# A two-block transformer kernel: the first attention's softmax parts, head ends, weight splits and adaptive-scale steps rearranged

## The chip, the cores and the metric

The kernel runs on one core of one Trainium2 chip. A core has a matrix engine (TensorE, PE in the profile; its weight loads are PEld), three engines for elementwise work (VectorE or DVE, ScalarE or ACT, GpSimd or POOL), a queue that only issues transfers (SyncE or SP) and 16 DMA engines. Each engine runs its own instructions in the order in which they were written and waits on semaphores for the others. The metric is the device time of one execution in microseconds: before, the median of three runs is 3294.83 us (3290.88 to 3296.75).

## What is computed

Two residual blocks over 2048 tokens of width 1024, all in float32. The change lies in the first:

```python
def first_block(x, ...):
    h = rmsnorm(x, norm_pre_g)
    q, k, v, g_attn, c_h, c_b, c_c, g_conv = split(h @ w_in)
    q, k = rope(q), rope(k)                      # 12 heads of 64
    # three windows: (128, step 1), (512, step 4), (2048, step 16), mixed by softmax of their log-sums
    o = sum_i softmax(lse)_i * dilated_window_attn(q, k, v, window_i, step_i)
    attn_out = o * silu(g_attn)
    conv_out = c_b * causal_depthwise_conv(c_c * c_h, conv_w) * silu(g_conv)
    x = x + rmsnorm(concat(attn_out, conv_out) @ w_out, norm_post_g)
```

The second block scales its norms by `silu(c) @ w_ada + b_ada` ("ada" below), then has a Fourier mix, a windowed attention and a mixture of 16 experts.

## The kernel before

Matrix products with float32 accuracy are made in one of two ways. Either both operands are cut into a rounded high part and a rest (`split`: ScalarE casts the high part, VectorE subtracts it), and the products of the parts are summed, or an operand is taken whole in float32.

**Stage A** makes the projections: `proj` is 24 products of 512 columns, four groups of tokens for each of 26 weight tiles. Between them, in the last 14 tiles, stand the ada steps: a step ends one pair of ada tiles (`Ada.end`: two small products that sum over partitions), cuts the sums of the pair before (`finish`), makes sums on VectorE (`sums`) and loads a tile. One step stands behind each group of products in tiles 0 to 8 of the 14, and two in three of the groups. What `end` multiplies was cut in the step before it. `Bias.heads` writes a 2 MB table out.

**Stage B** is the first attention, head by head (`phase_b`, 12 heads). The loop over heads holds 20 slots (`for k, ... in enumerate(ch)`), one for each chunk of up to 512 columns of the exponentials. In slot k PE transposes the chunk's four blocks into PSUM (`tpose`), then computes some scores of the next head (`score`: two products, and a VectorE instruction that adds the mask and takes the minimum); ACT makes exponentials (`expo`); `parts` brings the transposed chunk to SBUF; and PE multiplies by v the chunk of two slots before (`products(2)`, `mms`). `parts` has three ways, by a table `WHOLE` with one letter a chunk: H cuts into two parts (ACT and DVE), A and V copy the chunk whole (ACT or DVE). A whole chunk's product is one float32 instruction, a cut one's is two. Heads 0 to 10 copy 8 of 20 chunks whole, head 11 copies 7.

`total` gathers the sums of the exponentials of a head across partitions with 16 small copies on POOL (in the last head on DVE); `total2`, in slot 2 of the next head, adds, inverts, and at once transposes the inverse on PE. v is loaded in one layout and turned into the second on POOL (`turn_v`, 16 copies a head). POOL also repeats ka and kb to the other 64 partitions (`repeat`) and sorts q (`order`). The result T of a head has the sums of two halves in its upper and lower partitions: one half is stored, the other is added in DRAM by a POOL transfer (`rest`).

Heads 10 and 11 carry in addition the cuts of the eight 128x1024 tiles of `w_out` (`wo.split`: a copy and a subtraction of 1024 columns), four in each. Head 11 has no scores left to make; instead PE has the first 14 pieces of the output product (`fill`, 3 products of 512 columns each), whose left operand comes from loads (`out.loads`), multiplications on POOL and a cut (`out.mul`). Stage C begins with the other half of that product, for which nothing is missing, and then needs the next 256 tokens' operand, which `mix_loads(1)` and `mix_mul(1)` bring. All loads stand in SP's one queue.

Of the kernel before, what the change touches and what calls it, by code (L numbers as in the profile page):

```python
# [9 lines left out]
F32 = mybir.dt.float32  # L10
# [83 lines left out]
def prep(inp):  # L94
# [35 lines left out]
    "s_v": ([H1, 128, NT, 128], F32),  # L130
# [167 lines left out]
def phase_a(tc, A, K):  # L298
    nc = tc.nc
    ident, eps = K["ident"], K["eps"]  # L300
    with ExitStack() as es:
# [23 lines left out]
        with ExitStack() as e1:  # L325
# [74 lines left out]
            def v_store(t, vs):  # L400
                nc.sync.dma_start(A["s_v"][:, :, t].rearrange("h p d -> p h d"), vs.rearrange("p h a d -> p h (a d)").bitcast(F32))
# [184 lines left out]
        with tc.manual_schedule():  # L586
            last = None
            loads, sums = [], []
            na = 0

            def ada_step(more):
                nonlocal na
                ada.end()
# [11 lines left out]
            for i, j in enumerate(order):  # L605
                nxt = order[i + 1] if i + 1 < len(order) else None
                if i == 9:
# [5 lines left out]
                for n in range(4):  # L613
# [17 lines left out]
class QK:  # L631
# [10 lines left out]
    def open(self):  # L642
        self.add(1)
        with self.tc.using_default_side("right"):
            self.q2p = self.es.enter_context(self.tc.tile_pool(name="q2B", bufs=2, reuse_waits="tile"))
# [12 lines left out]
    def repeat(self, h, n, eng):  # L658

        t = self.T[h][n]  # L660
# [23 lines left out]
class Out:  # L684
# [19 lines left out]

    def mul(self, tiles, hl, ks, eng):
        raw, g, r = tiles
        if ks.start < 6:
            eng.tensor_mul(g[:, ks], g[:, ks], r[:, ks])
            eng.tensor_mul(raw[:, ks], raw[:, ks], g[:, ks])
        split(self.tc.nc, hl[0][:, ks], hl[1][:, ks], raw[:, ks])  # L710
# [15 lines left out]
def phase_b(tc, A, K):  # L726
# [5 lines left out]
    with ExitStack() as es:  # L732
# [18 lines left out]
        m2 = cp.tile([128, 512], F32, name="m2")  # L751
        HD = {}
# [3 lines left out]
        def load_v(h):  # L756
            v1, v2 = (vv[h % 2].tile([128, KC, 256], F32R, name=n).rearrange("p a b -> p (a b)") for n in ("ph", "pl"))
            v1, v2 = v1.rearrange("p (t d) -> p t d", d=128), v2.rearrange("p (c a d) -> p c a d", c=4, d=128)
            nc.sync.dma_start(v1.bitcast(F32), A["s_v"][h])
            HD.setdefault(h, {}).update(v1=v1, v2=v2)  # L760

        def turn_v(h, i):

            d, (c, u) = HD[h], divmod(i, 4)
            nc.gpsimd.tensor_copy(d["v2"][QD[u], c], d["v1"][QD[c], u::4].bitcast(F32))
# [44 lines left out]
        WHOLE = [{k: {"A": nc.scalar.copy, "V": nc.vector.tensor_copy}[e] for k, e in enumerate(w) if e != "H"} for w in ("HAHHAHHHHHAHVHVVHHVA", "VVHAVHVVHHVHHHHHHHHH")]  # L810
# [20 lines left out]
        def total(h):  # L831
            d = HD[h]
            L = d["den"]
            E = st.tile([128, 4, 4], F32, name="E2", bufs=2)
# [1734 lines left out]
```

## Time and profile before

| | |
|---|---|
| median of the runs (lowest to highest) | 3294.83 us (3290.88 to 3296.75) |
| the profiled execution: its own time, its span | 3293.63 us, 3291.8 us |
| PE busy | 3110.4 us, 94% of the span |
| DVE, ACT, POOL busy | 2021.7, 1437.4, 675.4 us (61%, 44%, 21%) |
| stage A until | 754 us |
| stage B: first scores, first slot of head 0, of head 10, of head 11 | 754, 772.0, 1079.4, 1112.6 us |
| last product of head 11, first product of the next tokens | 1157.9, 1179.3 us |

The page's shares are averages over the span. Four places matter here: the ada steps in stage A (430 to 630 us), the steady heads (772 to 1079), heads 10 and 11, and the seam to stage C (1158 to 1185).

### The profile page before, as it was taken

To read this page: it belongs to the slowest core of one execution; us is meant where nothing else is said; L and a number is where in the kernel's file an instruction comes from. 1 tells how busy PE (TensorE), PEld (TensorE's weight loads), DVE (VectorE), ACT (ScalarE), POOL (GpSimd) and SP (SyncE) were. 2 spreads that over 40 slices of the span, in tenths; PEclk is the share of its full clock that TensorE was granted. 3 is DMA by queue.
4 is the path that set the end of the run, shared out by engine and by line. 5 is a ranking of instruction groups with operands and counts; after the bars stand their busy time and mean duration, and the time that the engine had idled before them with its cause. 6 is when DMAs were issued, how large, how long until landed. Compare 5 with 4: busy or idle time off the path is not lost. (4 is left out here: it accounts for less than half of the span.)

```text
span 3291.8 us, 49939 instructions
## 1 busy us (share of the span) xinstructions
PE 3110.4 (94%) x19200; PEld 2766.1 (84%) x19200; DVE 2021.7 (61%) x4077; ACT 1437.4 (44%) x3072; POOL 675.4 (21%) x784
## 2 busy tenths in 40 slices
PE   9999999999999889789998999489999999999998
PEld 8988877888888767689986778389999999999997
DVE  5445557627888835547777476755565665565654
ACT  4322211105888723436657332244444444454443
POOL 0022210005566447311121010100110010010010
PEclk9999999999999999899999999789999999999999
DMA  5433357405555478544444765346666556665653
GB/s 167 138 132 122 117 184 233 142 20 143 148 126 142 117 218 232 140 132 154 146 139 153 235 187 175 129 180 212 211 211 213 205 205 212 211 217 206 208 203 102
DMA packets 200885, 556.83 MB, mean 169 GB/s; under 512 B 26512, under 2 KB 119580, under 8 KB 180294
## 3 DMA queue, kind: packets, MB, share of 16 engines
q1 hardware_dynamic: 186902, 499.73, 45.3%
q0 software_dynamic: 13456, 53.37, 7.0%
q8 instruction: 151, 2.47, 0.3%
q14 instruction: 88, 0.72, 0.1%
q10 hardware_dynamic: 288, 0.53, 0.0%
HBM read 425.29 MB, written 130.37 MB: 169 GB/s over the span
## 5 line engine op out<-in xcount | busy, mean ns | idle before, releaser
L2481 PE MATMUL mm<-xh,wh 128*128 128x256 f32 x2048 | 581.9, 284 | 0.2 <-ACT xh L188 0.2
L2481 PE MATMUL mm<-xl,wh 128*128 128x256 f32 x2048 | 580.7, 284 | 0.1
L2481 PE MATMUL mm<-xh,wl 128*128 128x256 f32 x2048 | 580.5, 283 | 0.0
L2475 DVE TENSOR_TENSOR wl<-raw,wh 128x1024 fp32r<-128x1024 f32 x380 | 453.8, 1222 | 177.0 <-ACT wh L2474 177.0
L2481 PEld LDWEIGHTS mm<-xh,wh 128*128 128x128 f32 x2048 | 394.2, 192 | 1.1 <-ACT xh L188 0.4
L2481 PEld LDWEIGHTS mm<-xl,wh 128*128 128x128 f32 x2048 | 394.1, 192 | 1.0 <-DVE xl L189 0.4
L2481 PEld LDWEIGHTS mm<-xh,wl 128*128 128x128 f32 x2048 | 394.1, 192 | 0.0
L2474 ACT CAST wh<-raw 128x1024 fp32r<-128x1024 f32 x384 | 390.1, 1049 | 0.0
L481 PE MATMUL mm<-hH,wl 128*128 128x512 f32 x832 | 325.2, 391 | 1.9 <-DVE wl L189 1.9
L481 PE MATMUL mm<-hH,wh 128*128 128x512 f32 x832 | 325.6, 391 | 0.0
L481 PE MATMUL mm<-hL,wh 128*128 128x512 f32 x832 | 325.4, 391 | 0.0
L2536 POOL DMA_INDIRECT out_dram<-yo,idx x32 | 63.1, 1973 | 750.7 <-DVE yo L2535 583.0
L829 ACT ACTIVATE s<-s,nm 128x256 f32<-128x256 f32 (+3 forms) x384 | 202.1, 531 | 19.5 <-DVE nm L824 19.5
L189 DVE TENSOR_TENSOR pl<-pt,ph 128x512 fp32r<-128x512 f32 (+1 forms) x269 | 176.6, 662 | 48.7 <-ACT ph L188 46.6
L2531 PE MATMUL y<-wh,hh 128*128 128x512 f32 x512 | 204.4, 399 | 0.0
L2531 PE MATMUL y<-wh,hl 128*128 128x512 f32 x512 | 200.1, 391 | 0.0
L2531 PE MATMUL y<-wl,hh 128*128 128x512 f32 x512 | 199.7, 390 | 0.0
L188 ACT CAST ph<-pt 128x512 fp32r<-128x512 f32 (+1 forms) x269 | 149.8, 562 | 110.4 <-PE pt L856 40.9
L481 PEld LDWEIGHTS mm<-hH,wl 128*128 128x128 f32 x832 | 157.2, 189 | 35.2 <-DVE wl L189 2.3
L481 PEld LDWEIGHTS mm<-hH,wh 128*128 128x128 f32 x832 | 157.1, 189 | 35.2 <-issue 1.7
L481 PEld LDWEIGHTS mm<-hL,wh 128*128 128x128 f32 x832 | 157.0, 189 | 32.2
L798 DVE CUSTOM_DVE_ANT_0 s<-ps,m 128x256 f32<-128x256 f32 (+3 forms) x384 | 156.9, 449 | 35.2 <-PE ps L797 33.8
(474 smaller groups left out, 6938.1 us busy)
## 6 DMA issues: line engine op xcount, KB each, us to landing
raw<-in_wg SPq DMA_DIRECT2D x32, 2048.0 KB
raw<-in_wd SPq DMA_DIRECT2D x32, 2048.0 KB
raw<-in_wu SPq DMA_DIRECT2D x31, 2048.0 KB
adaw<-in_wada SPq DMA_DIRECT2D x32, 768.0 KB
x<-in_x SPq DMA_DIRECT2D x32, 512.0 KB
wraw<-in_w1t SPq DMA_DIRECT2D x26, 512.0 KB
s_v<-vs SPq DMA_DIRECT2D x16, 768.0 KB
q<-s_q SPq DMA_DIRECT2D x12, 1024.0 KB
```

Source lines behind the costliest of these rows:

```text
L188: nc.scalar.copy(hi, src)
L189: (e or nc.vector).tensor_tensor(lo, src, hi.bitcast(F32), op=ALU.subtract)
L481: nc.tensor.matmul(p, a[:, k, :], b[:, k, tk], start=i == 0, stop=i == 3 * KC - 1)
L798: nc.vector.tensor_tensor_reduce(sv, p[:, :w], mask[:, mask.shape[1] - w:], 1.0, TOP, ALU.add, ALU.min, d["nm"][:, i:i + 1])
L829: nc.scalar.activation(sv, sv, AF.Exp, bias=d["nm"][:, i:i + 1], scale=-1.0, accum_out=d["den"][:, i:i + 1])
L2474: nc.scalar.copy(hi[:, c], RAW[i][:, c])
L2475: eng.tensor_tensor(lo[:, c], RAW[i][:, c], hi[:, c].bitcast(F32), op=ALU.subtract)
L2481: nc.tensor.matmul(p, a.rearrange("p (k f) -> p k f", k=KC)[:, k, w0:w0 + 128], b[:, k, :], start=i == 0, stop=i == 3 * KC - 1)
L2531: nc.tensor.matmul(ys[sl][:, cs], a[:, kk, sl * 128:sl * 128 + 128], b[:, k, cs], start=kk == 0 and j == 0, stop=kk == 7 and j == 2)
L2536: nc.gpsimd.indirect_dma_start(out=A["out"], out_offset=bass.IndirectOffsetOnAxis(ap=idx[:, sl:sl + 1], axis=0), in_=y, in_offset=None, co ...
```

## The change

- **ada**: one step a group in tiles 0 to 9, none doubled; `end` takes what was cut two steps before (`aged`). `Bias.heads` goes to tile 9.
- **v**: stored by four transfers a tile in the second layout, and loaded in both layouts (1 MB each a head, five transfers); `turn_v` is gone.
- **parts**: the table `PARTS` has new letters: P copies whole on ACT, Q on DVE, into a new tile `pw`, and POOL then cuts it (a cast and a subtraction). Heads 0 to 10: 12 H, 5 P, 3 Q, none whole. Head 11: 11 H, 6 Q, 3 A (whole). Products follow three slots later (`products(3)`), what follows a product one slot later (`leave`).
- **total** is 16 small products on PE in slot 2; `total2` (slot 3) adds and inverts on DVE; `total3` (slot 5) transposes.
- Scores are spread over 15 slots instead of 14; `repeat` comes in eight quarters; `q2` has one buffer instead of two; `rest` goes from slot 6 to slot 15 (9 and 6 in heads 10, 11); T is copied by DVE three times of four (before, ACT three times).
- **All eight weight cuts in head 11**, copies by ACT and DVE in turn, subtractions on DVE.
- **End of head 11**: PE adds T's halves (four products with `both`), so the POOL transfer and the x5 load go; the reciprocals are spread by two products. `fill` begins at slot 8, its last two pieces stand behind the loop. `mix_mul(1)` is on DVE.

```diff
-                if i == 9:
+                if i == 10:
@@ ada_step
-                ada.end()
+                if ada.late and aged:
+                    ada.end()
+                aged = bool(ada.late)
@@ stage A, after each group
-                    if i < 9 and i * 4 + n > 1:
-                        for _ in range(1 + (i in (2, 4, 6) and n == 0)):
-                            ada_step(na < 32)
-                        if i == n == 1:
+                    if i < 10 and i * 4 + n > 2:
+                        ada_step(na < 32)
+                        if i == 9 and n == 1:
                             bias.heads(ps)
@@ phase_b
-        WHOLE = [... for w in ("HAHHAHHHHHAHVHVVHHVA", "VVHAVHVVHHVHHHHHHHHH")]
+        PARTS = ("HPHPHPHPHHPHHQHHQHQH", "QHQAQHQHHQAHQHHHHHAH")
@@ total
-            for c in range(4):
-                for u in range(4):
-                    copy(E[QD[c], u, :], Lr[QD[u], 1, c, :])
+            for u in range(4):
+                for c in range(4):
+                    nc.tensor.matmul(E[QD[c], u, :], ident[:, QD[u]], Lr[:, 1, c, :], start=True, stop=True, skip_group_check=True)
@@ parts
+            if how in "PQ":
+                whole = pw[:, k // 2 % 4, :w]
+                (nc.scalar.copy if how == "P" else nc.vector.tensor_copy)(whole, p[:, :w])
+                nc.gpsimd.tensor_copy(hi[:, :w], whole)
+                nc.gpsimd.tensor_tensor(lo[:, :w], whole, hi.bitcast(F32)[:, :w], op=ALU.subtract)
+            else:
+                split(nc, hi[:, :w], lo[:, :w], p[:, :w])
@@ the loop over heads
-            LA, SC, JD = 1, 14, 1
+            LA, SC = 1, 15
-            L10, W10, W11 = (4, 13), (8, 9, 16, 17), (4, 6, 8, 10)
+            AT = {H1 - 2: 9, H1 - 1: 6}
+            W11, L11 = {0: 0, 1: 1, 3: 2, 5: 3, 7: 4, 9: 5, 12: 6, 16: 7}, {5: 6, 8: 7}
-            MU, FB = {4: slice(6, 8), 9: slice(0, 2), 10: slice(2, 4), 11: slice(4, 5)}, 6
+            TM = {6: slice(0, 2), 8: slice(2, 4), 10: slice(4, 5)}
+            MU, FB = {4: slice(6, 8), 9: slice(0, 2), 13: slice(2, 4), 15: slice(4, 5)}, 8
-                    products(2)
+                    products(3)
-                    if k == 2 and h:
-                        total2(h - 1)
-                    if k == 6 and h:
+                    if h and k in (2, 3, 5):
+                        (total, total2, None, total3)[k - 2](h - 1)
+                    if h and k == AT.get(h, 15):
                         HD[h - 1].pop("rest")()
@@ behind the loop
-            nc.vector.tensor_mul(x5, x5, g5)
-            split(nc, hl[0][:, 5], hl[1][:, 5], x5)
+            for q in range(4):
+                p = ps_t.tile([128, 512], F32, name="pt")
+                nc.tensor.matmul(p[own], both, T[:, q * 512:q * 512 + 512], start=True, stop=True)
+                if q == 0:
+                    nc.vector.tensor_mul(x5[own], p[own, :256], g5[own])
+                    split(nc, hl[0][:, 5], hl[1][:, 5], x5)
+                nc.scalar.copy(T[own, q * 512:q * 512 + 512], p[own])
+            nc.sync.dma_start(A["s_t"][5, own], T[own])
@@ mix_mul
-                out.mul(tiles, parts, slice(k, k + 2), nc.gpsimd)
+                out.mul(tiles, parts, slice(k, k + 2), nc.vector if pi == 1 else nc.gpsimd)
```

PE in slots 2 and 3 of head 5, before (pt: a transposed chunk, ps: scores, po: products with v):

```order
L876 MATMUL po<-pl,ph 128x256
L848 MATMUL pt<-ident,r 16x128
L856 MATMUL pt<-ident,s_7859 128x128 x4
L797 MATMUL ps<-ka,q_8132 128x512
L797 MATMUL ps<-kb,q_8132 128x512
L797 MATMUL ps<-ka,q_8132 128x128
L797 MATMUL ps<-kb,q_8132 128x128
L876 MATMUL po<-ph 128x256
L876 MATMUL po<-ph 128x128
L856 MATMUL pt<-ident,s_7859 128x128 x4
```

and the same engine there after the change, from slot 2 on:

```order
L853 MATMUL pt<-den,ident 32x4 x16
L871 MATMUL pt<-ident,s_8003 128x128 x4
L811 MATMUL ps<-ka,q_8352 128x384
L811 MATMUL ps<-kb,q_8352 128x384
L811 MATMUL ps<-ka,q_8352 128x512
L811 MATMUL ps<-kb,q_8352 128x512
L897 MATMUL po<-ph 128x256
L897 MATMUL po<-pl,ph 128x256
L897 MATMUL po<-ph 128x256
L897 MATMUL po<-pl,ph 128x256
```

The transposition of the inverse (`L848`) has left slot 2, sixteen small products stand there, and the products without a second row (a whole chunk) have become pairs.

POOL over one steady head, before (pl<-ph: `turn_v`, E<-den: `total`):

```order
L905 DMA s_t<-T 64x2048
L661 CAST ka<-ka 64x2048
L661 CAST kb<-kb 64x2048
L765 CAST pl<-ph 32x512 x2
L777 COPY q_8132<-q 128x512 x4
L765 CAST pl<-ph 32x512 x4
L839 COPY E_8250<-den 32x4 x16
L765 CAST pl<-ph 32x512 x10
```

and after, the middle of such a head (ph, pl<-pw: the cut of a P or Q chunk):

```order
L886 CAST ph<-pw 128x512
L887 TENSOR_TENSOR pl<-pw,ph 128x512
L667 CAST ka<-ka 64x512 x2
L886 CAST ph<-pw 128x256
L887 TENSOR_TENSOR pl<-pw,ph 128x256
L667 CAST kb<-kb 64x512 x3
L791 COPY q_9356<-q 128x512
L886 CAST ph<-pw 128x256
L887 TENSOR_TENSOR pl<-pw,ph 128x256
L667 CAST kb<-kb 64x512
L791 COPY q_9356<-q 128x512
L922 DMA s_t<-T 64x2048
```

The cuts stand between quarters of the repeats, so that PE's products now wait for POOL too.

SP's queue at the seam, before (s_t: the stored T; raw, g, r: the next tokens' operand):

```order
L902 DMA m_5772<-T 64x256
L904 DMA s_t<-T 64x2048
L697 DMA raw<-s_mix 128x2x256
L699 DMA g<-s_g 128x4x256
L702 DMA r<-s_r 64x4x256 x2
```

and after:

```order
L866 DMA s_r<-rt 16x128
L1110 DMA s_t<-T 64x2048
L703 DMA raw<-s_mix 128x2x256
L705 DMA g<-s_g 128x4x256
L708 DMA r<-s_r 64x4x256 x2
```

The store of T, which now holds the summed halves, stands ahead of the loads as the store of one half did before; the load of x5 from T is gone.

## Rows read from the trace of the kernel before

**Rows 1.** Windows: head 0 to 9, head 10, head 11; first row names columns.

```profile
core 0: us, PE busy (x) PEld busy (x) DVE busy (x) ACT busy (x) POOL busy (x), PEclk, DMA share, GB/s
772.00:1079.40 307.40, 293.81 (x2374) 263.72 (x2375) 259.87 (x896) 259.72 (x840) 205.25 (x410) 0.99 0.52 138
1079.40:1112.60 33.20, 29.81 (x239) 26.53 (x238) 29.08 (x94) 25.84 (x85) 15.94 (x28) 1.00 0.46 128
1112.60:1157.90 45.30, 36.20 (x193) 29.37 (x192) 31.80 (x60) 25.00 (x75) 19.70 (x18) 0.89 0.37 104
```

**Rows 2.** Timeline of PE in head 4: start, us, line, out<-in, idle before.

```profile
901.75 0.27 PE L848 MATMUL pt<-ident,r 128*16 128x128 f32 x1 [1.32 <-DVE r L846]
```

**Rows 3.** Timeline of PE: products of chunks whole (x4) and cut, and what follows.

```profile
904.68 0.28 PE L876 MATMUL po<-ph 128*128 128x256 f32 x1
...
905.15 0.60 PE L856 MATMUL pt<-ident,s 128*128 128x128 f32 x4
...
908.45 1.02 PE L876 MATMUL po<-ph 128*128 128x256 f32 x4
909.31 0.60 PE L856 MATMUL pt<-ident,s 128*128 128x128 f32 x4
...
916.49 0.34 PE L876 MATMUL po<-ph,pl 128*128 128x384 f32 x1
...
917.01 0.62 PE L856 MATMUL pt<-ident,s 128*128 128x128 f32 x4
...
919.98 1.03 PE L876 MATMUL po<-ph,pl 128*128 128x384 f32 x4
920.95 0.44 PE L818 MATMUL ps<-nm,ident 128*32 128x8 f32 x32
```

**Rows 4.** Lines of stage B: out<-in xcount, busy us, mean ns, idle before.

```profile
L765 POOL CAST pl<-ph 32x512 fp32r<-32x512 f32 x192 | 117.9, 614 | 64.4 <-DMA ph<-s_v 45.8 <-PE pt L848 6.5 <-PE po L876 3.2
L865 DVE COPY ph<-pt 128x512 f32<-128x512 f32 (+2 forms) x50 | 33.9, 678 | 4.8 <-PE pt L856 4.8
L839 POOL COPY E<-den 32x4 f32<-32x4 f32 x176 | 32.6, 185 | 36.9 <-ACT s L829 30.4
```

**Rows 5.** Timeline of POOL: a subtraction of 1024 columns; two `turn_v` copies beside a DVE copy.

```profile
1114.40 2.39 POOL L681 TENSOR_TENSOR kb<-T,kb 128x1024 fp32r<-128x1024 f32 x1
...
1120.65 2.51 POOL L765 CAST pl<-ph 32x512 fp32r<-32x512 f32 x2
```

**Rows 6.** Timeline of DVE in the same stretch (L680 copies weights, L681 subtracts).

```profile
1116.16 0.69 DVE L189 TENSOR_TENSOR pl<-pt,ph 128x512 fp32r<-128x512 f32 x1 [0.34 <-ACT ph L188]
...
1119.82 1.31 DVE L680 CAST q<-s 128x1024 fp32r<-128x1024 f32 x1
...
1125.42 0.68 DVE L680 CAST ka<-s 128x1024 fp32r<-128x1024 f32 x1
1126.14 1.22 DVE L681 TENSOR_TENSOR ka<-s,ka 128x1024 fp32r<-128x1024 f32 x1
```

**Rows 7.** Waits of PE, 440 to 640 us: who for whom, total, times, longest.

```profile
PE adap L290 <- ACT adah L188: 8.1, 2, 4.1
```

**Rows 8.** Windows (columns as in rows 1): behind each of those two waits.

```profile
464.00:472.00 8.00, 7.74 (x18) 4.42 (x18) 7.08 (x19) 2.13 (x3) 0.00 (x0) 0.57 0.80 244
501.20:506.00 4.80, 4.50 (x13) 3.38 (x14) 1.95 (x5) 1.43 (x2) 0.00 (x0) 0.64 0.97 244
```

**Rows 9.** Timeline of PE: its long waits in head 11 and at the seam.

```profile
1135.21 1.22 PE L716 MATMUL mm<-kb,ph 128*128 128x512 f32 x2 [4.42 <-ACT ph L188]
...
1151.14 0.37 PE L848 MATMUL pt<-ident,r 128*16 128x128 f32 x1 [3.28 <-DVE r L846]
...
1179.27 0.80 PE L716 MATMUL mm<-q,pl 128*128 128x512 f32 x1 [8.18 <-DVE pl L189]
```

**Rows 10.** Timeline of POOL at the seam.

```profile
1174.80 1.26 POOL L708 TENSOR_TENSOR g<-g,r 128x512 f32<-128x512 f32 x1 [9.20 <-DMA r<-s_r]
```

**Rows 11.** Window behind the wait at the seam (columns as in rows 1).

```profile
1179.20:1185.00 5.80, 5.73 (x14) 4.55 (x15) 3.84 (x4) 1.24 (x2) 4.44 (x3) 0.52 0.89 315
```

More of the change, by code (lines that the diff above doesn't have):

```diff
@@ L751, in phase_b @@
         m2 = cp.tile([128, 512], F32, name="m2")
+        both = cp.tile([128, 64], F32, name="both")
+        nc.vector.tensor_add(both, ident[:, :64], ident[:, 64:])
+        pw = QKs.pwp.tile([128, 4, 512], F32, name="pw")
         HD = {}
@@ L956, in phase_b @@
                 order(1, c, nc.gpsimd)
-            for i in range(16):
-                turn_v(0, i)
             EX = exps(0)
@@ L997, in phase_b @@
                     tl = [x.rearrange("p (k t) -> p k t", t=256) for x in (s12[0][:, :2048], s12[1][:, :1536], s12[1][:, 1536:3072])]
-                    for i in range(4):
-                        wo.load(OUT[4 + i], (s12[0][:, 2048:], s12[1][:, 3072:])[i // 2][:, i % 2 * D:(i % 2 + 1) * D])
-                    out.loads(0, tl, (slice(6, 8), slice(0, 4), slice(4, 5)))
+                    slots = [x[:, j * D:(j + 1) * D] for x in (s12[0][:, 2048:], s12[1][:, 3072:]) for j in range(2)]
+                    wo.load(OUT[2], slots[0])
+                    out.loads(0, tl, (slice(6, 8),))
+                    wo.load(OUT[3], slots[1])
+                    out.loads(0, tl, (slice(0, 4),))
+                    wo.load(OUT[4], slots[2])
+                    out.loads(0, tl, (slice(4, 5),))
+                    wo.load(OUT[5], slots[3])
                     x5, g5, r5 = m2[:, :256], m2[:, 256:], m1
@@ L1005, in phase_b @@
                 for k, (_, bl, mm, aft) in enumerate(ch):
-                    if more and k == SC + JD:
+                    if more and k == SC + 2:
                         joint2(h + 1)
@@ L1017, in phase_b @@
                         ne += 1
-                        if ne == 32:
-                            total(h)
-                    if more and j >= 17:
-                        for e in EX2[ne - 32:2 * (j - 17) + 1]:
+                    if more and j >= 18:
+                        for e in EX2[ne - 32:2 * (j - 18) + 1]:
                             e()
                             ne += 1
+                    leave()
                     pend.append((mm, parts(p, w, k, h), aft))
-                    products(2)
@@ L1037, in phase_b @@
[L1037 to L1049 removed]
+                        for i in KD.get(k, ()):
+                            QKs.repeat(h + 2, ("ka", "kb")[i // 4], nc.gpsimd, i % 4)
@@ L1050, in phase_b @@
+                        if k in QO:
+                            order(h + 2, QO[k], nc.gpsimd)
+                    if h == H1 - 2 and k == 12:
+                        T = op.tile([128, S], F32, name="T")
+                        for j in range(2):
+                            wo.load(OUT[j], T[:, j * D:(j + 1) * D])
                     if not more:
                         if k in W11:
-                            i = 4 + W11.index(k)
-                            wo.split(OUT[i], wo_tile(i), nc.vector.tensor_copy, nc.vector)
+                            i = W11[k]
+                            wo.split(OUT[i], wo_tile(i), (nc.scalar.copy, nc.vector.tensor_copy)[i % 2], nc.vector)
+                        if k in L11:
+                            wo.load(OUT[L11[k]], slots[L11[k] - 6])
+                        if k in TM:
+                            out.times(tl, TM[k], nc.gpsimd)
@@ L1054, in phase_b @@
                         if k in MU:
-                            out.mul(tl, hl, MU[k], nc.gpsimd)
+                            out.part(tl, hl, MU[k])
                         if k >= FB:
```

131 lines of the change are left out of this document (66 added, 65 removed).

## The prediction

> **What bounds the kernel now.** I read the windows first, one per stretch [rows 1]: in heads 0 to 9 PE works 293.8 of 307.4 us, DVE and ACT 260 each, POOL 205, at the full granted clock. A head takes 30.74 us; in it PE has 29.4 us of work, DVE and ACT 26.0, POOL 20.5. So PE is the bound of the steady heads, and what PE is spared is worth its full price until DVE is reached. Then I looked for the gaps of PE by its timeline. In a steady head there is one, of 1.32 us: the transposition of the inverse waits for DVE's reciprocal [rows 2]. In head 11 and at the seam there are three long ones, 4.42, 3.28 and 8.18 us [rows 9]. In stage A the waits of PE show 8.1 us in two pieces for the ada parts [rows 7]. Behind long gaps the clock stands between its two levels (1.2 and 2.4 GHz): 0.57 and 0.64 behind the ada gaps [rows 8], 0.52 behind the seam's [rows 11], 0.89 over head 11 [rows 1]; behind the 1.32 us gap of the steady heads it stays at 0.99. A long gap thus costs its length and, after it, the lost clock.
>
> **Ada steps.** The two waits come where `end` needs a cut that ACT has only just been given. Two steps' delay gives it at least one more group of 24 products, more than the longest wait of 4.1 us, so I take the waits as gone: 8.1 us. With them goes the slow clock: 8.0 x 0.43 = 3.4 and 4.8 x 0.36 = 1.7 us [rows 8]. Together 13.2, taken as 13. The new order lets ACT wait for the products of the pair before (one buffer for the parts); behind it on ACT stands the eviction of a group that PE has not finished by then, and PSUM has four banks, so it costs nothing; without that cover the gain falls to 8, or to 0 if the waits only move. The four v stores a tile and the later table of `Bias.heads` issue more or later transfers on SP and POOL, off PE's path; between a loss of 2 us and none, taken as none.
>
> **The steady heads.** Removed from PE's path: the 1.32 us gap [rows 2], since the sums are made in slot 2, the inverse in 3 and the transposition in 5. Products of chunks: a whole chunk of 384+128 columns holds PE from 919.98 to 920.95, 0.97 us, a cut one from 916.49 to 917.01, 0.52 us: 0.45 saved. Two times 256: 908.45 to 909.31, 0.86, against 904.68 to 905.15, 0.47: 0.39 saved [rows 3]. Of the eight whole chunks of a head three are 384+128 and one is 512 (taken like these: 4 x 0.45 = 1.8), one is twice 256 (0.39), and three have one 256 (half of it, 0.2 each: 0.6). Sum 2.8 us. Added to PE: 16 small products, as half of the 32 that take 0.44 us together [rows 3]: 0.2. PE's head becomes 30.74 - 1.32 - 2.8 + 0.2 = 26.8 us.
>
> What must follow that pace: DVE loses four whole copies and wins three (Q), and wins two T copies, each about 0.68 us [rows 4], one narrow: +0.4, so 26.4. ACT has one instruction less, 25.8. POOL loses 16 x 0.614 = 9.8 and 16 x 0.185 = 3.0 us [rows 4] and gets eight casts and eight subtractions over 3200 columns: subtractions at 2.39 us per 1024 [rows 5] are 7.5 us; for the casts the nearest row is a copy of 512 columns at 0.614 [rows 4], 6.25 of them 3.8 us; the quarters of the repeats perhaps 1 us. POOL: 20.5 - 12.8 + 11.3 + 1 = 20 us of 27. It has room, and its chain of some 2 us a chunk must end within three slots of about 1.35 us each, 4 us. So three engines lie within 1 us of each other. Their work is not even over the slots, and few buffers (three for transposed chunks, three for scores) couple them; the pace lies between 26.8 and 29.4, where only the gap is saved. I take 27.8, nearer to the sums, since before, with the same buffers, PE lost nothing outside the gap. Heads 0 to 9: 10 x (30.74 - 27.8) = 29.4, less 1.3 for head 0, which has no such gap: 28 us. The price without this cover is 1.6 us a head more.
>
> Here a page of the Trainium skill speaks against the change: "GPSIMD Engine Reference", section "Engine selection", says that elementwise work with two inputs belongs on VectorE, GpSimd being about twice as slow. The rows agree: 2.39 us for 1024 columns on POOL [rows 5] against 1.22 on DVE [rows 6]. By that rule the eight subtractions would stay on DVE, whose head would then be some 30 us, and of the 2.9 us a head little would be gained; by the sum above POOL's slowness is paid out of its idle time.
>
> **Head 10** loses its four weight cuts and its DVE load of 29.1 us [rows 1]: 33.2 to 27.8, 5.4 us.
>
> **Head 11** (to its last product, 45.3 us). PE's work is short there: 45.3 less the gaps of some 9 us (4.4 and 3.3 us [rows 9], and the first slots' one of the kind of [rows 2]), and at clock 0.89 less 45.3 x 0.11 = 5 us of slow clock, in part within the gaps. What fills it now is DVE: 31.8 us [rows 1], less four to six copies and subtractions of chunks, less the 16 copies of `total`, plus four more subtractions at 1.22 and, against T copies and multiplications, a little more: 33 to 34 us. The weight cuts read and write SBUF only, and beside POOL such a DVE copy took 1.31 us instead of 0.68 [rows 6]; POOL has six pairs and the multiplications, some 18 us. So DVE needs 33 to 40 us and I take the head at 40: 5 us saved. Bounds: 11 saved (34 us) and 2 lost (47). `rest` on POOL waits for the store of head 10, with the multiplications queued behind it, as before; the fill that waited 4.42 us for them now begins two slots later.
>
> **The seam.** Before, the next tokens' products start 21.4 us after the last product of head 11 (1157.9 to 1179.27), with 5.8 x 0.48 = 2.8 us of clock lost behind [rows 9, 11]. Then: two fill pieces and the T products lie in PE's way (four float32 products of 512 columns, each like a whole pair of rows 3, 0.9 us, 3.5 in all), T is stored some 6 us after the last product instead of 2, and the loads stand behind that store on SP. Their data came at 1174.80 [rows 10], 14 us after their issue, with T's accumulation in DRAM beside them that is now gone: estimate 10 to 14. On DVE two multiplications and the cut follow in about 2.7 us. The start comes 6 + 11 + 2.7 = 19.7 us after the last product, and PE, with 18 us of work to then, waits 2. Gain 21.4 + 2.8 - 19.7 - 0.5 = 4 us; bounds -1 and 9.
>
> **Sum.** 13 + 28 + 5.4 + 5 + 4 = 55.4. The profiled execution took 3293.63; minus 55.4 is 3238.2. The median lies 1.2 us above that execution: 3239.
>
> **Rivals.**
> (a) The heads find a new bound: DVE at 26.4, or the POOL chain that reaches PE late, holds them at 29 us. For it: three engines within 1 us. Against: before, PE at 29.4 lost nothing to DVE and ACT at 26.0. Heads 0 to 10 then give 16 + 4 instead of 33: 3252.
> (b) Slower than before: DVE shuts POOL out. Rows 5 show two casts of 0.614 in 2.51 us while DVE copies from SBUF to SBUF, a factor of two. If this held for POOL's 20 us of each head, POOL would be the bound at 40 us, 9 us a head over before: 11 x 9 = 99, less the 22 us of the other terms and the like: about 3371. It decides from the point where POOL takes 33 us a head (a factor of 1.65). Against: in the steady heads DVE's inputs come from PSUM, and POOL's subtraction at 1114.40 took its 2.39 us while such a DVE subtraction at 1116.16 took 0.69 [rows 5, 6].
> (c) Head 11 gains nothing: the weight cuts on DVE and POOL's cuts hold each other up throughout, 48 us instead of 40: 3247. The Trainium skill has this as a rule ("SBUF — State Buffer", section "Who interferes with whom"): a DVE instruction with two SBUF inputs, or in a two-port mode, and a GpSimd instruction that reads SBUF exclude each other. By it (c) would hold in head 11 and (b) would not in the steady heads; the rows agree on both.
> (d) The ada part doesn't do what it says, since the data of the first tiles come late whatever the step: 3252.
> (e) Head 11 and the seam run with hardly a wait and the heads at 27.0: 3222.
>
> **How the numbers follow.** Forecast (3227 to 3247) 0.54, (a) 0.20, (c) or (d) 0.12, (e) 0.08, (b) 0.03, something in between that takes the gain away 0.03. The range reaches from the better case to (a) and somewhat beyond, both together: 3219 to 3263. What this kernel's measurement can tell from no change is about 0.2%, 6.6 us: faster 0.95, same 0.02, slower 0.03.
>
> **What would show it.** Right: steady heads of 27.3 to 28.3 us in the windows, no wait of the inverse's transposition, no rows of PE waiting for the ada parts, clock at 1.0 from 440 to 640 us. Wrong: PE products that wait for POOL's `pl`, scores that wait for DVE in every slot, POOL cuts of clearly over 1.9 us for 512 columns, or a wait at the seam as long as 8 us. If the heads' pace is over 29 us, the term of 28 fails, and with it the forecast.

## The result, and the profile after

The changed kernel takes 3257.89 us (median of 4 runs, 3255.8 to 3260.84) against 3292.86 for the kernel before on the same chip: a ratio of 0.9893, with a 95% interval of 0.9876 to 0.991. Forecast were 3239 us, with a range of 3219 to 3263. So the change gave 35 us where 55 had been worked out. The profiled execution took 3255.92 us, with a span of 3254.1; set against the profile before (3291.8) it is 37.7 us shorter, and that difference is split by stage here:

| term of the forecast | forecast | measured | before, after (us) |
|---|---|---|---|
| ada steps: start to the first score | 13 | 3.5 | 754.6, 751.2 |
| first score to head 0 | 0 | 0.2 | 17.4, 17.1 |
| heads 0 to 9 | 28 | 26.7 | 307.4, 280.7 |
| head 10 | 5.4 | 5.4 | 33.2, 27.8 |
| head 11, to its last product | 5 | 0.4 | 45.3, 44.9 |
| seam: from there to the 193rd output product | 4 | -1.6 | 47.1, 48.7 |
| all behind it, unchanged | 0 | 3.1 | 2086.8, 2083.7 |

Windows of the changed kernel for heads 0 to 9, head 10, head 11 and the seam up to the wait answer to [rows 1] (the first row names the columns):

```profile
core 0: us, PE busy (x) PEld busy (x) DVE busy (x) ACT busy (x) POOL busy (x), PEclk, DMA share, GB/s
768.30:1049.00 280.70, 278.11 (x2660) 261.27 (x2661) 253.67 (x904) 255.77 (x824) 200.05 (x286) 0.99 0.72 192
1049.00:1076.80 27.80, 27.73 (x272) 26.06 (x271) 25.26 (x92) 25.23 (x82) 14.09 (x19) 1.00 0.57 162
1076.80:1121.70 44.90, 36.49 (x251) 29.66 (x252) 38.39 (x50) 28.60 (x84) 25.81 (x22) 0.85 0.53 129
1121.70:1144.30 22.60, 20.02 (x79) 13.53 (x79) 4.29 (x9) 3.78 (x7) 0.00 (x0) 1.00 0.58 131
```

In the heads PE is now busy for 278.1 of 280.7 us: it is the bound almost alone. In head 11 it is DVE that has grown, from 31.8 to 38.4 us, and the clock is at 0.85.

Two long waits of PE stand in stage A, one new and one longer (timeline of PE; in the kernel before the first was 1.89 us, and the two of [rows 7] are gone):

```profile
174.10 0.50 PE L485 MATMUL mm<-hH,wl 128*128 128x512 f32 x1 [4.39 <-DVE wl L189]
...
468.39 0.79 PE L485 MATMUL mm<-hH,wh 128*128 128x512 f32 x1 [4.53 <-ACT g L551]
```

ACT's timeline shows what the second waits for. ACT must evict a gate (`g`) from PSUM, but the gate's buffer is still being stored:

```profile
467.75 1.21 ACT L551 ACTIVATE g<-mm 128x512 f32<-128x512 f32 x2 [15.90 <-DMA s_g<-g]
```

In head 11, groups of DVE and of POOL by line (mean ns of one behind the busy time); the first two rows are the same subtraction of 1024 columns. Both of the first row began just behind a POOL subtraction and ran beside it:

```profile
L687 DVE TENSOR_TENSOR kb<-s,kb 128x1024 fp32r<-128x1024 f32 x2 | 4.6, 2278 | 0.0
...
L687 DVE TENSOR_TENSOR q<-s,q 128x1024 fp32r<-128x1024 f32 x2 | 2.5, 1226 | 0.1
```

```profile
L887 POOL TENSOR_TENSOR pl<-pw,ph 128x512 fp32r<-128x512 f32 x7 | 10.2, 1464 | 0.6
L886 POOL CAST ph<-pw 128x512 fp32r<-128x512 f32 x7 | 5.6, 798 | 7.7 <-DVE pw L885 7.7
```

(The seventh pair is head 10's last chunk.) Of the second row's two, one ran while POOL stood. The other began 0.13 us ahead of a POOL subtraction and kept its time, and there POOL's took 2.23 us instead of 1.28 (timelines of DVE and of POOL):

```profile
1094.04 1.23 DVE L687 TENSOR_TENSOR q<-s,q 128x1024 fp32r<-128x1024 f32 x1
```

```profile
1094.17 2.23 POOL L887 TENSOR_TENSOR pl<-pw,ph 128x512 fp32r<-128x512 f32 x1
```

Timelines of POOL and of ACT in the middle of head 11: the accumulation of head 10's result, the multiplications behind it, and ACT's cut of what they make:

```profile
1096.46 0.84 POOL L922 DMA_DIRECT2D s_t<-T  x1
1097.04 1.57 POOL L713 TENSOR_TENSOR s<-s 128x512 f32<-128x512 f32 x1
```

```profile
1100.33 0.62 ACT L188 CAST ph<-s 128x512 fp32r<-128x512 f32 x1 [4.36 <-POOL s L714]
```

At the seam, in the order of the chain: SP stores T, the reciprocals land for DVE, PE goes on (compare [rows 9, 10]):

```profile
1128.17 0.46 SPq L1110 DMA_DIRECT2D s_t<-T  x1
```

```profile
1141.34 0.69 DVE L713 TENSOR_TENSOR g<-g,r 128x512 f32<-128x512 f32 x1 [6.13 <-DMA r<-s_r]
```

```profile
1144.34 1.22 PE L728 MATMUL mm<-kb,ph 128*128 128x512 f32 x2 [2.62 <-ACT ph L188]
```

### The profile page after: what moved, and what is told of

It reads as the page before. It is cut to its first block, busy times and chain, and to the rows that moved or that the text cites. A ratio compares the mean times of both kernels' runs of the same rounds, so it can differ in the third digit from the quotient of the medians.

```text
span 3254.1 us, 50849 instructions
## 1 busy us (share of the span) xinstructions
PE 3092.5 (95%) x19596; PEld 2760.8 (85%) x19596; DVE 2018.8 (62%) x4081; ACT 1435.6 (44%) x3067; POOL 665.4 (20%) x652
## 5 line engine op out<-in xcount | busy, mean ns | idle before, releaser
L2577 POOL DMA_INDIRECT out_dram<-yo,idx x32 | 62.4, 1951 | 751.5 <-DVE yo L2576 584.9
L485 PEld LDWEIGHTS mm<-hH,wl 128*128 128x128 f32 x832 | 156.9, 189 | 38.4 <-DVE wl L189 5.6
```

The lines of the kernel that those rows point to most:

```text
L485: nc.tensor.matmul(p, a[:, k, :], b[:, k, tk], start=i == 0, stop=i == 3 * KC - 1)
L2577: nc.gpsimd.indirect_dma_start(out=A["out"], out_offset=bass.IndirectOffsetOnAxis(ap=idx[:, sl:sl + 1], axis=0), in_=y, in_offset=None, co ...
```

## The experiments

Three questions were open: why stage A gave 3.5 us and not 13, why head 11 gave nothing, and whether the seam could have given more. A fourth experiment sizes the term of the heads, which came out nearly as forecast. The experiments up to the seam are one execution each, so they are read by their stages; the last four runs have four or five.

### Stage A: the stores of v

```diff
-                a, u = divmod(t, 4)
-                for c in range(4):
-                    src = vs[c * 32:c * 32 + 32]...
-                    nc.sync.dma_start(A["s_v"][:, u * 32:u * 32 + 32, c, a]..., src)
+                nc.sync.dma_start(A["s_v"][:, :, t].rearrange("h p d -> p h d"), ...)
@@ load_v: the second layout
+            for u in range(4):
+                for c in range(4):
+                    nc.sync.dma_start(v2[QD[u], c].bitcast(F32), A["s_v"][h, c * 32:c * 32 + 32, u::4])
```

> The changed kernel, but v is stored by one transfer a tile as before the change; the second layout is made at loading, by 16 transfers a head instead of one. Theory (the 64 small stores are what stage A paid with): in the changed kernel they hold SP's queue until 169.3 us instead of 165.6, the queue of q and k stores then runs 4 and later 8.8 us behind, so the first two gate tiles are stored 8.5 us later and ACT, which waits for their buffers, lets PE run dry at 463.9. Without them: PE's gap at 169.7 falls from 4.39 to about 1.9 us, the lag of the q and k stores against the kernel before is under 1 us, the gap of 4.53 us at 463.9 is under 1 us, and the first score starts at 742 to 744 us instead of 751.2. Rival (the new ada order itself, or ACT's queue, makes the gap at 463.9): that gap stays above 3.5 us, first score at 747 to 749. The heads should keep their 28.1 us if the 16 loads hide, 28.5 or more if not.

Measured: 3253.95 us. The first score starts at 740.43 us. On the same chip a run with the changed kernel's stage A (the first of head 11, below) had it at 747.9, 7.5 us later. PE's waits in stage A are one of 2.18 us, and none near 464; the lag of the q and k stores behind the kernel before is gone (0.6 us early). Timelines of PE (the first score, here and in the run beside it; the wait) and of ACT:

```profile
740.43 0.30 PE L807 MATMUL ps<-ka,q 128*128 128x128 f32 x1 [1.12 <-POOL q L787]
```

```profile
747.91 0.30 PE L811 MATMUL ps<-ka,q 128*128 128x128 f32 x1 [1.11 <-POOL q L791]
```

```profile
171.15 0.50 PE L481 MATMUL mm<-hH,wl 128*128 128x512 f32 x1 [2.18 <-DVE wl L189]
```

```profile
458.53 1.21 ACT L547 ACTIVATE g<-mm 128x512 f32<-128x512 f32 x2 [15.87 <-DMA s_g<-g]
```

ACT waits as long for the gate's store as in the changed kernel, 15.9 us, but the wait ends at 458.5 instead of 467.8, before PE has run out of PSUM. The same wait stood in the kernel before, and ended there 0.7 us before PE came to stand at the ada product (ACT's timeline of before):

```profile
459.15 1.22 ACT L547 ACTIVATE g<-mm 128x512 f32<-128x512 f32 x2 [15.85 <-DMA s_g<-g]
```

One pair does not size the stores' price, since the stage varies. In the seven runs that have the changed kernel's stage A as it is, the first score starts between 745.4 and 751.5 us, on one chip alone at 745.4, 748.9, 749.9 and 751.5; in the three that store v by one transfer a tile, at 739.5, 740.0 and 740.4. So the price is 5 to 12 us, and it has two parts. Up to the 1201st product of the projections, near 440 us, it is 2 to 6 us. From there to the first score the stage takes 303.0 to 303.1 us with v stored by one transfer, and 307.5 to 310.3 in six of the seven. In the seventh (the second edit of head 11 alone, below) the gate's wait reached PE as 0.09 us only, without any edit of this stage, and the stretch takes 303.3. ACT's timeline there:

```profile
463.41 1.21 ACT L551 ACTIVATE g<-mm 128x512 f32<-128x512 f32 x2 [15.85 <-DMA s_g<-g]
```

The gate's wait thus costs 4 to 7 us where PE comes to stand, and nothing where ACT's wait ends in time.

The 16 loads of v did not hide everywhere: heads 0 to 9 kept 280.7 us, head 10 took 29.0 instead of 27.8, and head 11 46.6.

### Stage A: the gates' buffers

```diff
-                g = gp.tile([128, 512], F32, name="g")
+                if n == 0:
+                    U["g"] = vp2.tile([128, S], F32, name="uy"[j % 2])
+                g = U["g"][:, tk]
```

In the changed kernel:

> The changed kernel, but the silu gates of tiles 12 to 17 go into the two long tiles that lie idle then, so that ACT waits for no store of a gate. Theory (the gap of 4.53 us at 463.9 is ACT waiting for a gate's store): it falls below 0.5 us, the gap of 4.39 us at 169.7 stays, and the first score starts at 745 to 746.5 us instead of 751.2. Rival (the one buffer of the ada parts or the ada loads hold ACT): the gap stays at 3 us or more, first score after 749.

Measured: 3262.52 us; the first score at 747.73, 0.2 us earlier than in the run with the changed kernel's stage A on that chip, which is nothing beside the 6 us by which that stage varies. The wait for `g` is gone, as the theory said, but most of its price didn't come back: from the 1201st product to the first score it takes 306.9 us, where 303 is the time without a wait. PE waits 2.15 us some 12 us later, for a weight's cut that stands on DVE behind the sums of ada tiles that landed late (timeline of PE):

```profile
476.60 0.50 PE L485 MATMUL mm<-hH,wl 128*128 128x512 f32 x1 [2.15 <-DVE wl L189]
```

In the kernel before:

> The kernel before, with the same edit of the gates' buffers. Theory (there the ada parts were late for a reason of their own: the first ada tile landed at 456.4, its sums take 7 us, then the cut; ACT's wait for the gate store ended at 459.2 and lay beneath): both waits of the ada product stay at 3.5 to 4.5 us, first score within 1 us of 754.6. Rival (the gate stores were the common cause of all three gaps, and the ada order was never to blame): the waits at 459.9 and 497.1 fall below 1 us and the first score starts at 743 to 747.

Measured: 3305.18 us; the first score at 756.06. Both waits of the ada product are as they were (timeline of PE), so there they were ada's own, as the prediction had taken them:

```profile
464.06 0.34 PE L290 MATMUL adap<-adah,adao 128*1 128x384 f32 x1 [3.98 <-ACT adah L188]
...
502.08 0.34 PE L290 MATMUL adap<-adah,adao 128*1 128x384 f32 x1 [4.75 <-ACT adah L188]
```

### Head 11: two edits and both together

The first edit takes POOL's cuts out of head 11, the second moves POOL's multiplications ahead of the accumulation:

```diff
-        PARTS = ("HPHPHPHPHHPHHQHHQHQH", "QHQAQHQHHQAHQHHHHHAH")
+        PARTS = ("HPHPHPHPHHPHHQHHQHQH", "HHHAHHHHHHAHHHHHHHAH")
```

```diff
-            TM = {6: slice(0, 2), 8: slice(2, 4), 10: slice(4, 5)}
+            TM = {3: slice(0, 2), 4: slice(2, 4), 5: slice(4, 5)}
```

The first alone:

> The changed kernel, but in head 11 the seven chunks that DVE copies and GpSimd cuts (Q) are cut by ACT and DVE (H). DVE keeps as many instructions of the same length (0.69 instead of 0.68 us), ACT gets seven casts more (4 us), GpSimd loses 15.8 us. Theory (DVE and GpSimd hold each other up): the weight subtractions of 2.2 us fall to 1.2 except beside the multiplications, DVE's busy time falls from 38.4 to 32 to 34 us, and the head takes 38.5 to 41 us instead of 44.9. Rival (DVE has simply too much to do, or the head waits for ACT): the head stays at 43.5 us or more, with DVE's busy time at 37 or more, or with ACT above 34 us and PE waiting for exponentials.

(The table has six Q in head 11, not seven.) Measured: 3265.42 us, head 11 43.6 us. In four runs in which head 11 is as in the changed kernel and v is loaded as there it takes 43.0 to 45.7 us, so that is no gain. DVE's time fell to 34.0 us, with most subtractions at 1.2 us, and the head did not follow. The window of the head (columns as above), DVE's group, then POOL, ACT and PE in their timelines:

```profile
1074.40:1118.10 43.70, 33.55 (x253) 26.88 (x251) 33.95 (x51) 31.23 (x90) 10.51 (x10) 0.92 0.56 133
```

```profile
L687 DVE TENSOR_TENSOR kb<-s,kb 128x1024 fp32r<-128x1024 f32 x2 | 2.4, 1208 | 0.3 <-ACT kb L686 0.3
```

```profile
1095.09 0.84 POOL L922 DMA_DIRECT2D s_t<-T  x1 [17.85 <-DVE pl L189]
```

```profile
1099.46 0.62 ACT L188 CAST ph<-s 128x512 fp32r<-128x512 f32 x1 [5.39 <-POOL s L714]
```

```profile
1100.85 0.48 PE L871 MATMUL pt<-ident,s 128*128 128x128 f32 x1 [6.22 <-ACT s L844]
```

Read from the top: the accumulation can issue only at 1095.1, behind the store of head 10's result, which left SP at 1089.2 and on whose landing it waits too; the multiplications stand behind it on POOL; ACT stands 5.4 us before the cut of their product; the exponentials stand behind that cut on ACT; and PE waits 6.2 us for an exponential. The part of the theory on DVE held, the part on the head's time fell.

Both edits:

> As the run without GpSimd's cuts in head 11, and in addition GpSimd makes the multiplications of the output's operand in slots 3 to 5 instead of 6, 8 and 10, ahead of the accumulation of head 10's result, which it has to wait for. Theory (in that run ACT stood 5.4 us at the operand's cut, behind GpSimd's multiplications, which stood behind the accumulation that could start at 1095.1 only; the exponentials queued behind on ACT then left PE idle for 6.2 us): both waits go and head 11 takes 36.5 to 39 us instead of 43.6, with DVE at 32 to 34. Rival (DVE, or the loads of the operand, hold the head all the same): 41 us or more, with a gap of PE of 3 us or more somewhere else.

Measured: 3256.23 us; the window of head 11:

```profile
1075.70:1112.10 36.40, 31.95 (x252) 25.41 (x252) 33.28 (x50) 30.86 (x90) 11.99 (x10) 1.00 0.67 163
```

36.4 us, at a clock of 1.00, and no gap of PE over 1.3 us.

The second alone, with POOL's cuts kept:

> The changed kernel with GpSimd's cuts of seven chunks in head 11 kept, and only the multiplications moved to slots 3 to 5, ahead of the accumulation. Theory (two costs, the order on GpSimd and the mutual hold-up of DVE and GpSimd): PE's wait for the exponentials goes, but the weight subtractions stay at 2.2 us and DVE at 35 us or more: the head takes 40 to 43 us. Rival 1 (only the order on GpSimd matters): 37 to 39 us, as with the cuts gone. Rival 2 (the multiplications wait for their loads and now hold GpSimd's cuts up): 44 us or more, PE waiting for pl.

Measured: 3257.99 us, head 11 46.8 us, the second rival's case. POOL's multiplications fill 1086.8 to 1093.2 us without a break and hold its cuts up. The window, and PE's waits for POOL's parts (who for whom, total, times, longest):

```profile
1070.10:1116.90 46.80, 34.98 (x251) 28.93 (x252) 37.17 (x50) 28.74 (x84) 26.67 (x22) 0.89 0.51 125
```

```profile
PE po L897 <- POOL pl L887: 4.6, 5, 1.3
...
PE po L897 <- POOL ph L886: 3.5, 1, 3.5
```

So the two causes do not add: with POOL's cuts in place the order makes no gain (43.0 to 45.7, and 46.8), without them it makes 7.2 us (43.6 and 36.4, on two chips; the run with two queues below, with both edits, has 36.1).

### The heads: the worth of the cuts

```diff
-        PARTS = ("HPHPHPHPHHPHHQHHQHQH", ...
+        PARTS = ("HAHAHAHAHHAHHVHHVHVH", ...
```

> The changed kernel, but in heads 0 to 10 the eight chunks that GpSimd cuts are copied whole by ACT (5) and DVE (3) and multiplied in float32, as before the change. What is left of the change in a head is then the moved sums and reciprocal. Theory (PE is the bound and a cut chunk spares what the rows of both kernels show as a sum over a head, 12.1 against 10.3 us for all products): a steady head takes 29.7 to 30.2 us instead of 28.07. Rival (the price of my working, 2.8 us a head): 30.7 us or more. Rival (the cuts spare PE next to nothing, the whole gain is the gap of 1.32 us that went): below 28.8.

Measured: 3278.41 us, a steady head 29.02 us. Windows of heads 1 to 9, first with whole chunks, then the changed kernel's:

```profile
794.10:1055.30 261.20, 261.20 (x2432) 241.86 (x2431) 231.08 (x820) 232.05 (x739) 70.08 (x117) 1.00 0.72 183
```

```profile
796.00:1049.00 253.00, 250.60 (x2431) 235.46 (x2432) 230.20 (x820) 230.04 (x741) 182.94 (x262) 1.00 0.70 188
```

The result lies between the theory and its second rival. Of the 2.6 us that a steady head gained (heads 1 to 9: 30.68 to 28.11), POOL's cuts make 0.91 and the moved sums and reciprocal, with the rest of the new order, 1.7. And with whole chunks PE never waits at all, while with POOL's cuts it idles 0.27 us a head.

### The seam

```diff
                 nc.scalar.copy(T[own, q * 512:q * 512 + 512], p[own])
-            nc.sync.dma_start(A["s_t"][5, own], T[own])
+                if q == 0:
+                    nc.sync.dma_start(A["s_t"][5, own, :512], T[own, :512])
+            nc.scalar.dma_start(A["s_t"][5, own, 512:], T[own, 512:])
```

> The changed kernel, but the summed halves of head 11 are stored in two pieces: the first 512 columns, which hold all that the next tokens need, by SP right after their copy, the rest by ACT's queue, so that SP comes to the next tokens' loads 1.5 to 2 us earlier. Theory (the chain store, loads, multiplications, cut sets the seam): from the last product of head 11 to the 103rd output product it takes 20.5 to 21.3 us instead of 22.6, PE's wait there shrinks from 2.6 to 1 us or less. Rival (the reciprocals' loads take until 19 us after the last product whatever their issue, since the DMA engines are the limit): 22.3 us or more.

Measured: 3257.61 us; from the last product (1119.2) to the 103rd output product (1140.9) 21.7 us, half way between theory and rival, and PE's wait there 1.64 us. Timelines of SP and of DVE:

```profile
1123.94 0.46 SPq L1111 DMA_DIRECT2D s_t<-T  x1
```

```profile
1137.48 0.69 DVE L713 TENSOR_TENSOR g<-g,r 128x512 f32<-128x512 f32 x1 [5.92 <-DMA r<-s_r]
```

From the store's issue to the reciprocals it is 13.5 us here, 13.2 in the changed kernel, and 15.0 before (1159.77 to 1174.80): the loads take their time wherever they start. T was stored 4.7 us after the last product instead of 6.5, and the seam became 0.9 us shorter: an earlier start brings at most its own length. The three later runs with this edit have 21.4 to 21.5 us.

### The three gains together

> The changed kernel with three edits of the runs so far together: v stored by one transfer a tile, head 11 without GpSimd's cuts and with the multiplications first, the early store at the seam. If the gains add (stage A 7 to 10 us, head 11 7 to 8 us, seam 0.5 to 1, less 1 us in head 10 for the 16 loads of v), the time is 14 to 18 us below the changed kernel: 3240 to 3244 us. If they don't (head 11's wait moves into the seam, where loads take 13 us from the store of T whatever came earlier), only stage A's share is left: 3248 us or more.

> The same, but v is stored in the second layout by four transfers a tile as in the changed kernel, two of them on ACT's queue and two on SP's. Theory (the lag of stage A comes from the time that SP takes to issue 64 small stores, 1.2 us each, at the end of the v tiles): half of it goes, the load of the tables leaves SP 4 us earlier, PE's gap at 463.9 is under 1.5 us and the first score starts at 741 to 745; head 10 keeps 27.8 us, since v needs no 16 loads. Rival (the transfers themselves are the cost, 32 partitions at a time): the first score at 747 or later, with the gap at 463.9 of 2.5 us or more.

> The changed kernel itself once more, on the chip of the two runs beside it, so that their stages and times can be set against it: 3255 to 3261 us, first score between 745 and 752 us, head 11 between 43 and 47 us.

Measured, on one chip: 3242.81 us with the three edits (ratio to before 0.9841, interval 0.9828 to 0.9855), 3249.53 with v stored by two queues (0.9863, 0.9848 to 0.9878), 3257.9 for the changed kernel (0.989, 0.9875 to 0.9905). The first score starts at 739.5, 750.5 and 749.1 us.

The gains of stage A and of head 11 add, though not in full, and the version with all three beats both kernels. The stores' theory fell: with half of the stores on ACT's queue the tables' loads leave SP at 166.1 instead of 169.3, and PE still waits 4.40 us at 169 and 4.76 at 463. So it is not the issuing that costs, but the transfers. Windows of 100 to 140 us and 166 to 172 us, first of the kernel before, then of the changed one, then the second window of the run with two queues (the last two columns are the DMA share and GB/s):

```profile
100.00:140.00 40.00, 40.00 (x245) 39.84 (x243) 18.67 (x43) 14.39 (x33) 0.00 (x0) 1.00 0.46 137
166.00:172.00 6.00, 4.11 (x19) 3.11 (x18) 1.39 (x4) 1.88 (x2) 0.00 (x0) 1.00 0.99 323
```

```profile
100.00:140.00 40.00, 40.00 (x244) 39.84 (x243) 18.55 (x43) 14.67 (x33) 0.00 (x0) 1.00 0.61 136
166.00:172.00 6.00, 3.71 (x17) 2.74 (x15) 0.51 (x2) 1.38 (x2) 0.00 (x0) 1.00 0.85 149
```

```profile
166.00:172.00 6.00, 2.80 (x13) 1.99 (x11) 0.23 (x4) 1.65 (x2) 0.00 (x0) 1.00 0.99 183
```

The same bytes (137 and 136 GB/s from 100 to 140 us) take a third more of the DMA engines' time when a tile is stored in four pieces of 32 partitions. Packet by packet, a store of v consists of packets of 512 bytes, and in that stretch one of them occupies its DMA engine for 29 ns (median) in the kernel before, and for 45 ns in the changed kernel and in the run with two queues. The 6 us from 166 on show the outcome and not the price, since they don't move the same: of the tables' packets of 8 KB, 141 fall into them before, 13 after the change and 38 with two queues.

With all three edits head 11 takes 41.3 us, and 36.1 in the run with two queues, which loads v as the changed kernel does. In the former ACT waits for a weight's load (its timeline), and the loads of v stand ahead of these in SP's queue:

```profile
1084.65 1.05 ACT L682 CAST q<-s 128x1024 fp32r<-128x1024 f32 x1 [3.06 <-DMA s<-in_wo]
```

The last run moves the loads of v behind the store of head 9's result:

```diff
-                if more:
+                if more and h < H1 - 2:
                     load_v(h + 1)
@@ slot 5
+                    if h == H1 - 2 and k == 5:
+                        load_v(h + 1)
```

> As the run with the three edits together, but in head 10 the 17 loads of head 11's v stand in SP's queue behind the store of head 9's result instead of ahead of it. Theory (in that run these loads held SP for 11 us at the start of head 10; the store, the accumulation behind it and so the first loads of the output weights came 5 us late, and in head 11 ACT stood 3.1 us before a weight's copy, with the exponentials behind it): the first weight load leaves SP about 21 us after the start of head 10 instead of 26, head 10 takes 27.8 to 28.3 us instead of 28.8, head 11 takes 36 to 38.5 instead of 41.3, and the time is 3236 to 3240 us instead of 3242.8. Rival (the DMA engines are full there, whatever the order: 0.99 to 1.00 of their time in the first half of head 11 in both runs): head 11 stays at 40 us or more and the time at 3241 to 3245.

Measured: 3243.58 us (0.9843, 0.9829 to 0.9856), the same as without. Head 10 takes 27.8 us, as the theory said, but the first weight load leaves SP 24 us after its start, since the 17 loads now stand directly ahead of it, and head 11 takes 39.6. What holds it there, SP's queue or the full DMA engines, stays open.

## Why the prediction held in total, and where it didn't

**Heads 0 to 9 and head 10** (33.4 forecast, 32.1 measured) carried the result. The pace of 27.8 us became 28.1, the wait of the inverse's transposition is gone, and POOL's time of 20 us a head came out at 20.3. But the working behind the number was off in two places that cancelled. The products were priced at 2.8 us a head from four hand-picked pieces of [rows 3]; summed over all products of a head, the time from one instruction's start to the next falls from 12.1 us to 10.1, or 10.3 with PE's waits for POOL, and the run with whole chunks makes the pace 0.91 us slower. The sixteen small products take 0.37 us a head, not 0.2, and the scores 0.4 more than before. And no engine held PE up, for which 1.0 us a head had been added: PE's own work is 27.8 us, not 26.8, and it idles 0.27. Rival (a), 29 us a head, did not happen; that the run with whole chunks has this pace is chance, since there PE holds it and not DVE or POOL.

Rival (b) did not happen. The two casts of 2.51 us that it started from [rows 5] ran beside the end of DVE's copy and, for most of their time, beside a DVE subtraction with two SBUF inputs (1121.17 us, 1.51 us long), of which the steady heads have none. In the steady heads POOL's cut of 512 columns takes 0.61 and 1.29 us (groups of POOL, heads 1 to 9), 1.9 us together, the figure that the text had named as the limit:

```profile
L887 POOL TENSOR_TENSOR pl<-pw,ph 128x512 fp32r<-128x512 f32 x36 | 46.5, 1291 | 2.9
...
L886 POOL CAST ph<-pw 128x512 fp32r<-128x512 f32 x36 | 22.1, 613 | 34.6 <-ACT pw L885 33.3 <-DVE pw L885 0.6
```

**The ada term** was right as far as it went. Stage A of the run with v stored as before differs from the kernel before in the ada steps alone, and its first score is 14.2 us earlier (754.6 to 740.4, two chips; forecast 13). What failed is the sentence beside it, that the v stores cost between 2 us and nothing: they cost 7.5 and 9.6 us in the two pairs on one chip each (740.4 against 747.9, 739.5 against 749.1), and 5 to 12 over all runs. They delay the tables, the q and k stores run 4 and then 8.8 us late, the gates' stores with them, and so the four PSUM banks of the projections, which the text had named as the cover, ran out after all. For the same reason the sign "clock at 1.0 from 440 to 640 us" was missed by a little: it is 0.99, and 1.00 in the run with v stored as before. The working had counted SP's issues, but not how much of the DMA engines' time a store takes. The Trainium skill has a rule that would have asked for that: "SBUF — State Buffer", section "Door 1: The DMA port swizzle (why [64,N] ≈ [32,N])", says that a transfer's bandwidth depends on how many of SBUF's 16 ports its partitions reach, and that 32 neighbouring partitions reach eight. By that rule a store in quarters is slower than one of 128 partitions; the trace agrees in direction (45 ns a packet against 29). That it is the ports, and not something else in which the two stores differ, no run separates.

**Head 11** was sized at 40 us and took 44.9, within the bounds of 34 and 47, and near rival (c). Its mechanism was there: subtractions of 1.22 us took up to 2.3 beside POOL, and DVE's 38.4 us lie at the upper end of the 33 to 40 of the working. The rule that (c) cites from the Trainium skill, that a DVE instruction with two SBUF inputs and a GpSimd one that reads SBUF exclude each other, agrees with both stretches: head 11 shows it and the steady heads, where DVE reads PSUM, do not. Two steps failed. The first is "What fills it now is DVE": freed of 4.4 us of DVE's time, the head still took 43.6. The second is "with the multiplications queued behind it, as before": the order accumulation, multiplications, cut, exponentials runs over POOL and ACT, and it was known as a wait of the fill of 4.42 us [rows 9]. Two slots' delay of the fill was taken as its cure, while the cut in front of the fill still stood in ACT's queue at slot 9. Neither is the whole cause: only with POOL's cuts gone and the order changed did the head become shorter (36.4), and with the cuts in place PE waited 8.1 us for POOL's parts.

**The seam** was sized at +4, with bounds of -1 and 9, and came out at -1.6, just outside them. PE's wait fell from 8.18 to 2.62 us, as forecast (2). But the step "6 + 11 + 2.7" became 6.5 + 13.2 + 3.0, since the loads take 13 us without the accumulation in DRAM as well; and PE's own work to there (T's halves at 3.7 us, the spread reciprocals at 0.65, two fill pieces) came to 20.0 us, not 18. Nor did the slow clock go with the long wait: 1.6 us were lost to it behind the wait (a mean of 0.94 over 26.0 us to the 193rd product), where the sum had left 0.5. The waits of the output's pieces behind it, 0.79 and 1.74 us against 0.88 before, took the rest.

**The rest** gave 3.1 us in code that is unchanged. It can't be claimed for the change: the stage named in the last section varies by more.

The sum was too large by 17.7 us: 9.5 in stage A, 1.3 in the heads, 4.6 in head 11 and 5.6 at the seam, less 3.3 that came unforeseen. The time lies outside the band of the main forecast (3227 to 3247) and inside the range only because that reached to rival (a) and beyond, and rival (a) is not what used the room up: stage A, head 11 and the seam did. The heads' term was right by two errors that cancelled. That part of the agreement is luck.

## What to carry to other kernels

When a step is moved off an engine, look for the waits that cost nothing yet, and for how much delay they bear: ACT's 15.9 us for the gate's store stood in the profile before and cost PE nothing, with the old ada order or the new one, until stores 9 us late made it PE's. An engine with idle time is worth loading where its results come in time: GpSimd's cuts paid in the steady heads, where DVE reads PSUM and PE idles 0.27 us a head, and in head 11, where DVE reads SBUF and GpSimd has the multiplications as well, they stood in the way of 7 us. How much of that is DVE and GpSimd holding each other up, and how much GpSimd's full queue, no run separates. And where a cut or copy waits for a slow engine, the whole queue behind it waits too, so the slow engine's work belongs early.

## What the runs showed of the hardware

The stage behind the output product, the same in every kernel here, takes 510 to 518 us from run to run, with the same instructions. The granted clock is 0.97 in the shortest and 0.95 in one of the longest, and 0.01 of 510 us is 5 us. Between the kernel before and the changed one the clock takes 18.8 and 15.4 us of the stage, 3.4 of the 3.7 us by which they differ. Over all runs length and clock go together only roughly (512.9 us at 0.96, 513.6 at 0.97), and what lets the clock return earlier in one run stays open. Windows of the kernel before, of the changed kernel, and of the run with both edits of head 11:

```profile
1356.40:1870.50 514.10, 467.86 (x2963) 430.69 (x2962) 346.37 (x832) 275.47 (x694) 96.22 (x107) 0.96 0.47 152
```

```profile
1322.70:1833.10 510.40, 465.77 (x2962) 428.82 (x2961) 345.91 (x833) 275.06 (x695) 96.68 (x107) 0.97 0.47 153
```

```profile
1316.60:1833.30 516.70, 470.65 (x2962) 432.79 (x2962) 348.13 (x834) 275.51 (x695) 96.79 (x107) 0.96 0.47 152
```

A gain of 4 us in one stage must therefore be read from that stage, not from the total of one run, and against several runs in which the stage is unchanged: stage A alone varies by 6 us on one chip.
